# RWKV's output products grouped by tile form, its gram products by turns into two banks of a shared PSUM pool

## The chip, the cores and the metric

One core of a Trainium2 chip runs the program. The metric is the time of one execution on the device in microseconds (us). The kernel before was run three times; one more execution was profiled, and all rows below are from that one.

## The reference

One layer of a hybrid backbone over 2048 latent tokens and 256 context tokens, width 1024: adaLN and norm, one input projection, three token mixers side by side (gated DeltaNet, RG-LRU, RWKV-7; each in both directions over the tokens), one output projection, a squared-ReLU FFN. All in fp32. The mixer that the change touches is RWKV-7, 6 heads of 64 channels, where per token and head the state S (64x64) goes by

```python
def step(S, xt):
    w, kk, a, k, v, r = xt
    S = (S * w[:, :, None, :]
         - jnp.einsum('bhvk,bhk->bhv', S, kk)[..., None] * (kk * a)[:, :, None, :]
         + v[..., :, None] * k[:, :, None, :])
    y = jnp.einsum('bhvk,bhk->bhv', S, r)
    return S, y
```

DeltaNet (GDN below) has a recurrence of the same kind; its keys and queries are normalised per head, and its decays come from gates.

## The kernel before

The kernel runs in four stretches: `front` (the normed tokens h in DRAM, and RWKV's operands), then `middle` with two chains one after the other, then the FFN. The change is in the first half of `middle`: `rwkv_mixer` beside `gdn_features`.

**RWKV's chain.** The recurrence is taken in chunks of 64 tokens, 36 steps per direction, both directions (dd 0 and 1) beside each other. Of a pair of heads each has 64 of the 128 partitions (`half[par]`), so six heads are 3 pairs r by 2 parities par. Per direction and step there are:

- `gram(dd, n)`: loads `pk` (4 operands of 64 tokens per head), and multiplies them with each other: per parity three products of 64 rows, 128 columns each, into a bank `rg` (one PSUM bank, pool `rpg`, one buffer). VectorE takes from it `am` and `zl` (masked), ScalarE `mu`, the matrices to be inverted. 8 grams (4 steps) make a round of 24 units.
- `Lanes.invert`: the inverses of a round, 60 small VectorE operations (`ltmp`, `yl`) in a row between transposes (`ml`, `x`, `y`), and small products (`lmc`, `lmy`) in a bank of the pool `rpl`.
- `load(dd, n)`: `kbr`, scaled on GpSimd and transposed on TensorE to `kbn`.
- `step(dd, n)`: three dependent products in banks `rps` (pool `rpc`, two buffers): z from the state `s` and `zl`, copied to `zz`; u from the inverse `y` and `zz`, copied to `uv`; `ds` from `kbn` and `uv`, added on VectorE to the decayed state `se`. From step 4 on the output follows, `rout` (pool `rpl`): per pair and parity a product of the state `s` with `rt` (a part of `kbr`), 64 rows, and one of `uv` with `am`, 128 rows, summed in PSUM; ScalarE copies it to `o`.

`chains` sets their order: grams up to 16 half-steps ahead, an inverse's parts among the steps of the round before.

**GDN's features.** `gdn_features` streams h three times (keys, queries, values; 9 pieces of 256 tokens) past columns of the input projection: per tile of 128 columns 24 products into a bank `proj` (pool of two), each fp32 operand split in two parts (`hh`, `hl`; `whi`, `wlo`). Then a convolution and SiLU (`gy`), norms over heads by a product with ones (`gssq`), transposes to rows (`nps`). Beside them run `gates`, `decays` (`gdps`, `dm`, `edm`) and `ada_rest` (`adw`, `adps`). Their small products share the pool `gss`, two banks under the tag `sm`.

`weave` sets the two beside each other as the program is written down: half a part of the features to each part of the chain, and what is left of them after the chain. A scheduler then lays the instructions out per engine, each engine taking its own in that fixed order, and hands out the buffers of the pools. The lines of the profile: matmuls are issued by a helper (L156), VectorE's by L130, L135 and L138, ScalarE's activations by L108. PSUM has 8 banks: here 1 (`rpg`), 1 (`rpl`), 2 (`rpc`), 2 (`proj`), 2 (`gss`).

Of the kernel before, what the change touches and what calls it, by code (L numbers as in the profile page):

```python
# [7 lines left out]
F32 = mybir.dt.float32  # L8
# [12 lines left out]
T = SEQ + CTX  # L21
# [16 lines left out]
def poff(p):  # L38
    """column of a piece (256 tokens and its halo) in the padded h."""
    return 0 if p == 0 else 259 + 256 * (p - 1)  # L40


# scratch arrays in DRAM: name -> (shape, dtype)
# [26 lines left out]
class K:  # L70
    """one kernel's context: engines, inputs, scratch, constants."""
# [22 lines left out]
    def col(self, v):  # L94
        """a [128,1] column of a constant."""
        if v not in self.cols:
            t = self.const.tile([128, 1], F32, name=f"col{len(self.cols)}")
            self.G.memset(t, v)
            self.cols[v] = t
        return self.cols[v]  # L100
# [13 lines left out]
    def after(self, a, b):  # L114
        """a comes after b on their engine"""
        self.tc.add_manual_dep(a, b.name, mybir.DependencyInfo(
            mybir.DependencyClass.NoSync, mybir.DependencyReason.DATA), reason="order")

    def table(self, name):
        """the activation tables of what follows, up to the next call; what came before stays before."""  # L120
# [19 lines left out]
    def rms(self, pool, ss, n, eps):  # L140
        """[128, 1]: (ss / n + eps) ** -0.5, by Newton's steps from a guess by the exponent's bits"""
# [16 lines left out]
    def params(self):  # L158
        """vectors over channels as columns: rows of 128 loaded, then transposed by TensorE."""
# [31 lines left out]
# ---------------------------------------------------------------- adaLN modulation and h  # L191
def ada_first(k, pp, tag):
    """silu(c), shift and scale of the mixers' norm as columns, for latent (0) and context (1) tokens."""
# [36 lines left out]
def ada_part(k, j, q, w):  # L230
    """columns of chunk j of ada_w: their products with silu(c) in two sums over 512 rows, yet to be summed over
    the partitions. w: [128, 4, ADA_W] twice"""
# [12 lines left out]
def ada_row(k, j, q, w, acc, ps, gain, out):  # L245
    """the columns with their bias, times a gain, in every partition"""
# [9 lines left out]
def ada_rest(k, p, pp, tag):  # L256
    """scale and shift of the FFN's norm as columns; the mixers' gate times their post norm's gain as rows. In parts."""
# [23 lines left out]
def make_h(k, w, pp, tag):  # L281
    """norm of the tokens, scaled and shifted, channels on partitions. In parts, a piece each, after one that loads the first."""
# [44 lines left out]
# ---------------------------------------------------------------- the input projection  # L327
def split(k, e, src, raw, hi, lo):
    """src -> hi + lo = src exactly, of float32r, by way of raw"""
# [6 lines left out]
class Proj:  # L336
    """tiles of 128 columns of w_in, split in two float32r parts, and pieces of h streamed past them."""
# [8 lines left out]
    def weight(self, i, c0, m):  # L346
        """tile i: m columns from c0; it takes the place of the tile i before"""
# [9 lines left out]
    def raw(self, dtype):  # L357
        """what is to be split, and the second parts of h"""
        return self.hp.tile([128, self.u, PW], dtype, name="hl", bufs=self.lb)

    def weights(self, cols):
        """cols: (first column, how many) of each tile"""
# [4 lines left out]
    def passes(self, sets):  # L367
        """(set, piece, h): every set of tiles past all pieces. After the last piece a tile gives way to the next set's."""
# [13 lines left out]
    def load(self, p):  # L382
        """h of piece p and its halo, in units of channels, each split in two parts."""
# [13 lines left out]
    def parts(self, f, h, a=0, b=PW):  # L397
        """feature tile f of this piece: PSUM [m, b-a]. In parts."""
# [10 lines left out]
    def products(self, ps, f, h, kk, a, b):  # L409
        """what 128 channels of h add to feature tile f"""  # L410
# [5 lines left out]
    def feats(self, fs, h, a=0, b=PW):  # L416
        """several feature tiles beside each other, so that h's first channels are done with early"""
# [7 lines left out]
def drain(parts):  # L425
    """all parts of a computation; what it returns"""
# [7 lines left out]
def rsq(k, out, ps, scale, eps):  # L434
    """out = (scale * ps + eps) ** -0.5"""
# [4 lines left out]
def to_rows(k, pool, work, dst, src, tag):  # L440
    """src [128 (head parity, channel), 3 pairs, 256 tokens] -> rows: dst [(head parity, token of a chunk), 4 chunks,
    (pair, channel)] in DRAM, odd heads first."""
# [11 lines left out]
def backwards(k, rows):  # L454
    """rows(direction) [(head parity, token of a chunk), ...] in DRAM: the second direction's, from the first's"""
# [4 lines left out]
def gdn_features(k, es):  # L460
    """GDN's operands, in passes over h: keys, queries, values. In parts."""
# [5 lines left out]
    sm = es.enter_context(tc.tile_pool(name="gss", bufs=2, space=PSUM, side="right"))  # L467
# [6 lines left out]
    def normed(p, y, sq, s):  # L474
        """divided by the heads' norms; both orders of tokens"""
# [56 lines left out]
def lru_features(k, rec):  # L532
    """RG-LRU's inputs and output gates. In parts."""
# [13 lines left out]
def gdn_gates(k):  # L547
    """twice GDN's output gates. In parts."""
    N = 4
    with ExitStack() as es:  # L550
# [3 lines left out]
        for _, p, h in pj.passes([[(C_Z + 128 * j, 128) for j in range(3)]]):  # L554
            for j in range(3 if p else 0):
# [4 lines left out]
                # together, for the functions of RG-LRU are of other tables by turns  # L560
# [12 lines left out]
def turns(*parts):  # L573
    """parts of several computations by turns"""
# [4 lines left out]
def rwkv_out(k, w, pp, tag):  # L579
    """group norm over the heads, gain and bias, bonus, gate. In parts, by turns without functions of tables and with  # L580
    logarithms and powers."""
# [34 lines left out]
def gates(k):  # L616
    """Rows over tokens, of the heads and directions: (0) the decay's sums gc in chunks of 64, (1) exp(last gc - gc),
    (2) beta, (3) exp(gc). 256 tokens on a partition; the second direction's rows run backwards within each chunk. In parts."""
# [9 lines left out]
    def put(a, dd, x):  # L628
        """the second direction's rows run backwards within each chunk."""
# [1207 lines left out]
```

## Time and profile before

| what | us |
|---|---|
| three runs | 4391.04, 4398.76, 4412.45 |
| median | 4398.76 |
| span of the profiled execution, first to last instruction | 4383.5 |
| PE busy in the span | 3780.3 |
| DVE busy in the span | 2514.7 |
| GpSimd (POOL) busy in the span | 1702.6 |
| ScalarE (ACT) busy in the span | 1632.1 |

The profiled execution's own time is not given apart from its span; the median of the runs lies 15.3 us above that span. PE is TensorE's matmuls, PEld its weight loads, which run beside them; busy time is a union, so instructions that overlap count once. PEclk in a window is the granted clock as a share of 2.4 GHz. In the rows a name as `rout<-kbr,s` reads: written tile, then what is read; idle time before an instruction stands in brackets with what ended it.

### The profile page before, as it was taken

The page shows a single profiled execution, that of the slowest core. Times are in us where ns is not written, and L with a number is a line of the kernel's source. Part 1 is how long each engine was busy: PE and PEld are TensorE (multiplying, and loading weights), DVE is VectorE, ACT ScalarE, POOL GpSimd, SP SyncE. Part 2 cuts the span into 40 slices and gives each one's busy share as a digit, 9 for nine tenths or more (in the row PEclk, how much of TensorE's full clock was granted, in tenths as well). Part 3 has the DMA queues.
Part 4 walks back from the last instruction along what each step waited for, and adds up shares of the span by engine and source line. Part 5 has one row for each costly group of instructions (what it writes and reads, how often), then busy time and mean ns, then how long its engine had stood idle before and what let it go on. Part 6 is the DMA issues. An engine that isn't in the chain of part 4 may idle for free. (4 is left out here: it accounts for less than half of the span.)

```text
span 4383.5 us, 73864 instructions
## 1 busy us (share of the span) xinstructions
PE 3780.3 (86%) x28210; PEld 3119.3 (71%) x28210; DVE 2514.7 (57%) x4815; ACT 1632.1 (37%) x3393; POOL 1702.6 (39%) x1701
## 2 busy tenths in 40 slices
PE   5778786889999897867768768979999999999998
PEld 3667675777778676657556547768888887888886
DVE  3556455686787755329997996643333337333334
ACT  3443443454546433323355534542222214121212
POOL 3323233344356433445558564522233215121212
PEclk8888887888789777879788759989999999999999
DMA  7444446445556554454446465652121214111112
GB/s 208 122 111 110 106 105 172 121 137 149 153 158 197 169 148 127 142 164 119 122 118 189 128 192 152 196 173 64 59 60 60 63 44 151 48 53 44 53 44 82
DMA packets 561887, 527.52 MB, mean 120 GB/s; under 512 B 105069, under 2 KB 515326, under 8 KB 560382
## 3 DMA queue, kind: packets, MB, share of 16 engines
q1 hardware_dynamic: 556414, 506.02, 39.9%
q0 software_dynamic: 5120, 16.78, 1.3%
q8 instruction: 223, 3.65, 0.4%
q14 instruction: 130, 1.06, 0.1%
HBM read 396.87 MB, written 143.49 MB: 123 GB/s over the span
## 5 line engine op out<-in xcount | busy, mean ns | idle before, releaser
L156 PE MATMUL proj<-hh,whi 128*128 128x258 f32 (+2 forms) x2040 | 655.0, 328 | 113.1 <-ACT hh L392 58.7
L156 PE MATMUL proj<-hl,whi 128*128 128x258 f32 (+2 forms) x2040 | 650.2, 321 | 4.2 <-POOL hl L130 4.1
L156 PE MATMUL proj<-hh,wlo 128*128 128x258 f32 (+2 forms) x2040 | 639.0, 315 | 1.2 <-DVE wlo L130 1.2
L130 DVE TENSOR_TENSOR facc<-facc,fdn 128x512 f32<-128x512 f32 x480 | 326.1, 686 | 401.4 <-PE fdn L156 401.4
L156 PEld LDWEIGHTS proj<-hh,whi 128*128 128x128 f32 x2040 | 433.5, 216 | 152.7 <-ACT hh L392 62.7
L156 PEld LDWEIGHTS proj<-hl,whi 128*128 128x128 f32 x2040 | 439.5, 216 | 31.3 <-issue 16.4
L156 PEld LDWEIGHTS proj<-hh,wlo 128*128 128x128 f32 x2040 | 438.9, 216 | 18.0 <-issue 12.2
L130 POOL TENSOR_TENSOR hl<-hl,hh 128x520 fp32r<-128x520 f32 x216 | 291.0, 1353 | 383.3 <-ACT hh L392 293.2
L156 PE MATMUL fup<-fhh,uhi 128*128 128x512 f32 x1024 | 405.1, 396 | 7.5 <-DMA fhr<-h 4.3
L156 PE MATMUL fup<-fhl,uhi 128*128 128x512 f32 x1024 | 403.9, 395 | 0.8 <-DVE fhl L130 0.6
L156 PE MATMUL fup<-fhh,ulo 128*128 128x512 f32 x1024 | 403.8, 394 | 0.0
L156 PE MATMUL fdn<-dhi,ah 128*128 128x512 f32 x1024 | 399.2, 391 | 4.4 <-ACT ah L1743 1.8
L156 PE MATMUL fdn<-dlo,ah 128*128 128x512 f32 x1024 | 399.1, 390 | 0.0
L156 PE MATMUL fdn<-dhi,al 128*128 128x512 f32 x1024 | 395.0, 390 | 0.3 <-DVE al L130 0.3
L130 POOL TENSOR_TENSOR dlo<-draw,dhi 128x1024 fp32r<-128x1024 f32 x32 | 77.5, 2422 | 562.5 <-ACT dhi L331 562.5
L331 ACT CAST dhi<-draw 128x1024 fp32r<-128x1024 f32 x64 | 67.1, 1049 | 567.7 <-PE fdn L156 512.9
L130 POOL TENSOR_TENSOR fq<-fr 128x512 f32<-128x512 f32 x128 | 151.7, 1186 | 325.6 <-ACT fr L108 324.8
L130 DVE TENSOR_TENSOR ltmp<-yl,ml 128x30 f32<-128x30 f32 (+14 forms) x480 | 241.4, 503 | 10.6 <-DVE lu L135 0.8
L130 DVE TENSOR_TENSOR yl<-yl,ltmp 128x30 f32<-128x30 f32 (+14 forms) x480 | 238.6, 497 | 9.1
L156 PEld LDWEIGHTS fup<-fhh,uhi 128*128 128x128 f32 x1024 | 193.2, 189 | 52.7 <-ACT fhh L331 8.7
L392 ACT CAST hh<-hl 128x520 fp32r<-128x520 f32 x216 | 131.2, 623 | 261.4 <-DMA hl<-ht 253.3
L130 DVE TENSOR_TENSOR al<-fq,ah 128x512 fp32r<-128x512 f32 x128 | 93.6, 732 | 234.5 <-ACT ah L1743 234.1
(363 smaller groups left out, 8255.8 us busy)
## 6 DMA issues: line engine op xcount, KB each, us to landing
hl<-ht SPq DMA_DIRECT2D x144, 260.0 KB
uraw<-in_ffn_up_dram SPq DMA_DIRECT2D x64, 512.0 KB
draw<-in_ffn_down_dram SPq DMA_DIRECT2D x64, 512.0 KB
pk<-pk SPq DMA_DIRECT2D x72, 384.0 KB
kbr<-pk SPq DMA_DIRECT2D x72, 288.0 KB
hl<-ht SPq DMA_DIRECT2D x36, 520.0 KB
pk<-pk SPq DMA_DIRECT2D x72, 192.0 KB
pk<-pk SPq DMA_DIRECT2D x18, 768.0 KB
```

The costliest lines, as they stand in the source:

```text
L130: return e.tensor_tensor(out=out, in0=a, in1=b, op=op)
L156: self.last = self.PE.matmul(out, l, r, start=start, stop=stop).ins
L331: k.A.copy(hi, raw)
L392: k.A.copy(hh[:, x, :], raw[:, x, :])
```

## The change

Three things. (1) In `step`, the output's products are written in two groups, first the six of the state (64 rows), then the six of the values (128 rows); the first of the bank starts its sums, the others add where nothing was written since. (2) In `gram`, both parities' banks are taken first, and the products are written by turns between the parities; the readers follow after. (3) The pool `rpg` (one bank) and the pool `gss` (two banks) become one pool `msm` of three banks, opened in `middle`, in which a gram's two banks and all of GDN's small products have the tag `sm`. Comments and docstrings fall away too.

```diff
-def gdn_features(k, es):
+def gdn_features(k, es, sm):
...
-    sm = es.enter_context(tc.tile_pool(name="gss", bufs=2, space=PSUM, side="right"))
...
-def rwkv_mixer(k, es, ln):
+def rwkv_mixer(k, es, ln, psg):
...
-    psg = es.enter_context(tc.tile_pool(name="rpg", bufs=1, space=PSUM))
...
-        ges = []
-        for par in range(2):
+        ges = [psg.tile([128, 3, 128], F32, name=f"rg{par}", tag="sm") for par in range(2)]
+
+        for r in range(3):
+            for h, ge in zip(half, ges):
+                k.mm(ge[:, r, :], pk[h, r, 1:3, :].rearrange("p a t -> p (a t)"), pk[h, r, 0:4:3, :])
+        for par, ge in enumerate(ges):
             h, o = half[par], half[1 - par]
             A.copy(zl[h, par], pk[h, :, 0, :])
-            ge = psg.tile([128, 3, 128], F32, name="rg")
-            for r in range(3):
-                k.mm(ge[:, r, :], pk[h, r, 1:3, :].rearrange("p a t -> p (a t)"), pk[h, r, 0:4:3, :])
-            ges.append(ge)
...
             for r in range(3):
                 for par in range(2):
                     h = half[par]
-                    k.mm(out[h, r, :], s[h, par, r, :], rt[h, r, :], True, False)
-                    k.mm(out[h, r, :], uv[:, par, r, :], am[:, par, r, :], False, True)
+                    k.mm(out[h, r, :], s[h, par, r, :], rt[h, r, :], r == 0, False)
+            for r in range(3):
+                for par in range(2):
+                    k.mm(out[half[par], r, :], uv[:, par, r, :], am[:, par, r, :], False, r == 2)
...
-            weave(k, rwkv_mixer(k, es, ln), gdn_features(k, es), rates[0])
+
+            sm = es.enter_context(k.tc.tile_pool(name="msm", bufs=3, space=PSUM))
+            weave(k, rwkv_mixer(k, es, ln, sm), gdn_features(k, es, sm), rates[0])
```

The built programs show what became of it. PE's order at RWKV's last output, before and then with the change (`s` is the state, `uv` and `am` the values and their matrix):

```order
L156 MATMUL rps<-uv,kbn 64x64 x6
L156 MATMUL proj<-hh,whi_16506 128x260
L156 MATMUL rout<-kbr,s_15452 64x64
L156 MATMUL rout<-am,uv 64x64
L156 MATMUL rout<-kbr,s_15452 64x64
L156 MATMUL rout<-am,uv 64x64
```

```order
L156 MATMUL rps<-uv,kbn 64x64 x6
L156 MATMUL rout<-kbr,s_15449 64x64 x6
L156 MATMUL rout<-am,uv 64x64 x6
L156 MATMUL proj<-hl,whi_12359 128x260
L156 MATMUL proj<-hh,wlo_12360 128x260
```

The two forms stood by turns and now stand in blocks of six. In the new program all 64 outputs have the six of a form before the six of the other; in 37 nothing stands between.

PE's order among the first grams, before and then with the change (the numbers behind rg tell the two banks of a gram apart):

```order
L156 MATMUL rg<-pk 128x128 x6
L156 MATMUL rps<-kd_5694,ork 128x256 x3
L156 MATMUL rg<-pk 128x128 x6
L1439 MATMUL rps<-ident,kbr 128x128 x6
L156 MATMUL rps<-s_5818,zl 64x64 x6
```

```order
L156 MATMUL rg_6072<-pk 128x128
L156 MATMUL rg_6073<-pk 128x128
L156 MATMUL rg_6102<-pk 128x128 x3
L1437 MATMUL rps<-ident,kbr 128x128 x3
L156 MATMUL rg_6103<-pk 128x128 x3
L1437 MATMUL rps<-ident,kbr 128x128 x3
L156 MATMUL rps<-s_5818,zl 64x64 x6
```

Some grams stand by turns, others as three and three with other work between. Of the 72 grams 23 stand by turns (11 of these with nothing between), 48 as three and three, one mixed.

POOL's order behind the last `kbr` of RWKV's chain, before and then with the change (`hl` is the second part of h for proj; `edm`, `dm` are of the decays, `adw` of the modulation; `lx` belongs to the next half of `middle`):

```order
L130 TENSOR_TENSOR kbr<-kbr,wend 128x3x128
L130 TENSOR_TENSOR hl<-hl,hh 128x520 x2
L130 TENSOR_TENSOR se_15585<-s_15438,wend 64x192 x2
L130 TENSOR_TENSOR se_15598<-s_15452,wend 64x192 x2
L130 TENSOR_TENSOR hl<-hl,hh 128x520 x4
L938 MEMSET lx_18138 128x2
```

```order
L130 TENSOR_TENSOR kbr<-kbr,wend 128x3x128
L130 TENSOR_TENSOR se_15460<-s_15311,wend 64x192 x2
L130 TENSOR_TENSOR edm<-dm,neg 128x3x4x64
L236 DMA adw_16107<-in_ada_w_dram 128x4x128
L130 TENSOR_TENSOR hl<-hl,hh 128x520
L130 TENSOR_TENSOR adw_16106<-adw_16106 128x128
L130 TENSOR_TENSOR se_15582<-s_15435,wend 64x192 x2
L130 TENSOR_TENSOR hl<-hl,hh 128x520
L130 TENSOR_TENSOR adw_16106<-adw_16106 128x128
L130 TENSOR_TENSOR dm<-dm,cols 128x768
```

Features that stood among RWKV's steps now stand behind them. Counted over PE's order, proj products ahead of the first product of step 5 are 540 before and 336 with the change (those of the features alone), from there to step 35 1524 and 961, and behind the last rout and ahead of GDN's first gram 126 and 895. Behind the last kbr and ahead of GDN's chain POOL has 56 hl, 54 adw, 14 edm, 13 dm, 17 loads of adw and 4 gsq now.

## Rows read from the trace of the kernel before

**Rows 1.** the page: span and instructions

```profile
span 4383.5 us, 73864 instructions
```

**Rows 2.** windows of all engines; columns: stretch, length, busy (instructions), PEclk, DMA share, GB/s

```profile
706.00:873.00 167.00, 112.68 (x833) 96.48 (x834) 105.19 (x215) 74.81 (x166) 70.11 (x81) 0.72 0.54 150
873.00:977.50 104.50, 90.11 (x934) 78.03 (x934) 85.85 (x181) 53.30 (x122) 50.52 (x62) 0.87 0.48 143
977.50:1500.00 522.50, 492.77 (x4656) 412.18 (x4654) 384.39 (x841) 268.41 (x594) 266.47 (x311) 0.84 0.57 168
1500.00:1865.00 365.00, 300.34 (x2840) 250.04 (x2838) 186.31 (x400) 130.72 (x280) 139.88 (x163) 0.75 0.47 137
1865.00:1910.00 45.00, 28.76 (x204) 24.75 (x204) 12.16 (x26) 13.82 (x24) 16.55 (x16) 0.73 0.58 174
```

**Rows 3.** the same windows, instructions on rout alone (PE, PEld, ACT)

```profile
977.50:1500.00 522.50, 125.76 (x864) 88.72 (x864) 11.44 (x36) 0.84 0.57 168
1500.00:1865.00 365.00, 90.89 (x578) 63.93 (x578) 7.66 (x24) 0.75 0.47 137
```

**Rows 4.** the same windows, instructions on proj alone (PE, PEld, DVE, ACT)

```profile
977.50:1500.00 522.50, 175.67 (x972) 149.73 (x970) 52.99 (x115) 17.32 (x37) 0.84 0.57 168
1500.00:1865.00 365.00, 109.49 (x552) 93.79 (x552) 30.68 (x67) 10.87 (x23) 0.75 0.47 137
```

**Rows 5.** timeline of PE, 1868 to 1872 us; columns: start, us, instruction

```profile
1868.01 0.56 PE L156 MATMUL rps<-zz,y 64*64 64x64 f32 x12
1868.51 0.57 PE L156 MATMUL rps<-uv,kbn 128*64 128x64 f32 x12
1868.90 0.28 PE L156 MATMUL rout<-am,uv 128*64 128x64 f32 x2
1869.11 0.33 PE L156 MATMUL rout<-kbr,s 64*64 64x64 f32 x2
...
1871.42 0.33 PE L156 MATMUL rout<-am,uv 128*64 128x64 f32 x2
```

**Rows 6.** timeline of PE at 1167 us, granted clock 0.50

```profile
1167.41 1.54 PE L156 MATMUL rps<-zz,y 64*64 64x64 f32 x20
1168.87 0.58 PE L156 MATMUL proj<-hh,whi 128*128 128x260 f32 x1
```

**Rows 7.** timeline of PE at 1883 us, granted clock 0.50

```profile
1883.13 0.47 PE L156 MATMUL rout<-kbr,s 64*64 64x64 f32 x2
...
1887.97 0.59 PE L156 MATMUL proj<-hl,whi 128*128 128x260 f32 x1
```

**Rows 8.** windows of all engines around these timelines, columns as in rows 2

```profile
1166.70:1168.90 2.20, 2.20 (x25) 1.86 (x24) 2.06 (x5) 0.45 (x1) 0.00 (x0) 0.50 0.48 124
1883.10:1887.90 4.80, 4.80 (x25) 3.43 (x24) 2.06 (x5) 0.70 (x2) 2.07 (x2) 0.50 0.27 76
1868.00:1872.00 4.00, 4.00 (x49) 3.19 (x49) 1.05 (x3) 0.31 (x1) 0.00 (x0) 1.00 0.57 173
```

**Rows 9.** instructions on tile zz and on tile o: count, ns, first and last start

```profile
L1456 DVE COPY zz<-rps x72: 310/357/360, 753.9 to 1865.3; 128x192 f32<-128x192 f32 x72
...
L1487 ACT COPY o<-rout x64: 297/318/326, 969.7 to 1888.1; 128x192 f32<-128x192 f32 x64
```

**Rows 10.** timeline of DVE at 977.5 us: the eleventh of the copies to zz

```profile
977.46 0.34 DVE L1456 COPY zz<-rps 128x192 f32<-128x192 f32 x1
```

**Rows 11.** waits of PE, 706 to 1910 us: us in total, times, longest

```profile
PE rg L156 <- ACT mu L1411: 72.0, 27, 14.3
```

**Rows 12.** groups of POOL, 706 to 1910 us: busy, mean ns, idle before

```profile
L130 POOL TENSOR_TENSOR hl<-hl,hh 128x520 fp32r<-128x520 f32 x109 | 144.6, 1327 | 157.8 <-ACT hh L392 105.9 <-PE proj L156 16.3 <-ACT gy L108 15.4
...
L130 POOL TENSOR_TENSOR adw<-adw 128x128 f32<-128x128 f32 x144 | 72.4, 512 | 59.8 <-ACT adw L108 56.3
...
L130 POOL TENSOR_TENSOR edm<-dm,neg 128x768 f32<-128x768 f32 x18 | 33.0, 1836 | 0.3
...
L130 POOL TENSOR_TENSOR dm<-dm,cols 128x768 f32<-128x768 f32 x18 | 27.7, 1536 | 23.5 <-DMA dm<-gb 12.5 <-DVE cols L719 10.9
```

## The prediction

> **What bounds the kernel now.** The span is 4383.5 us [rows 1]; the median of the three runs, 4398.76, lies 15.3 above it, and the sum below is made against the span. I read the windows by stretch first. The changed code runs from 706 us, where RWKV's first gram products start, to 1910, where the last of GDN's features is written. What stands before is the same on every engine; what stands after has the same work, slightly interleaved anew. In 706 to 1910 PE is the busiest engine: 94% of 977.5 to 1500 and 82% of 1500 to 1865, against 74% and 51% for DVE [rows 2]. There, then, PE's time is worth nearly its own length, as long as no other engine is as full.
>
> Two things share PE here: RWKV's chain of 36 steps and GDN's features (proj). Two copies to zz mark a step; the first stands at 753.9, the eleventh (step 5) at 977.5, the last two at 1865 [rows 9, 10]. So 30 steps take 887 us, 29.6 each, with 793 us of PE [rows 2], 26.4 a step; 3.1 is idle.
>
> Then the timeline of one output event. A logical fp32 product is two matmuls. Written with the state's product (64 rows) and the values' product (128 rows) by turns, at the full clock (granted 1.00, 2.4 GHz [rows 8]) each logical product takes (1871.42 - 1869.11) / 9 = 0.257 us. Right before it, two groups of the same two forms, six logical products each, take 0.50 (64 rows) and 0.39 us (128 rows) up to the next start [rows 5]. At granted 0.50, which is 1.2 GHz [rows 8], the twelve by turns take 1887.97 - 1883.13 = 4.84 us [rows 7], while one grouped form goes at 1.46 / 20 = 0.073 us a matmul [rows 6].
>
> **The change, part by part.**
>
> *Output products grouped.* An event is 3.08 us at the full clock now (12 x 0.257), 4.84 at half. Grouped it is two blocks of twelve matmuls: at most 2 x 0.50 = 1.0, and at half 24 x 0.073 = 1.75. The 1442 matmuls of rout in the two large windows are 60 events and 216.7 us [rows 3], 3.6 each, which lies 30% of the way from 3.08 to 4.84. So an event becomes 0.7 x 1.0 + 0.3 x 1.75 = 1.23: a saving of 2.4 per event, 4.75 a step (two directions), 142 us in the 30 steps. The new order keeps the blocks whole: in 37 of 64 events all twelve logical products stand together, in every one the six of a form come first.
>
> *Gram by turns.* The by-turn order survives scheduling in only 23 of 72 grams; elsewhere three of one head stand, then three of the other. What two 64-row halves gain by overlapping at 128 columns no row shows. I take nothing; the other bound is half of these products' time, 23 x 12 matmuls x about 0.06 = 15 us. The Trainium skill, "TensorE: Matmul & The Clock Gate", Part 3 on packing, says that weight loads overlap running matmuls only where the row group differs, which is this case in those 23 grams; by it the sum would be those 15 us lower. No row of the trace decides it, and the sum goes without it.
>
> *Two banks for a gram.* Now the second head waits until the first head's readers (am, zl, mu) are done: PE lost 72.0 us in 27 such waits, 2.7 each [rows 11]. With two banks of three this goes, but the pool is shared: a gram takes two, so GDN's small products (gssq, nps, gdps, adps) often find one bank or none. Their matmuls then wait on PE for a gram's readers, with proj and the chain's products queued behind. Bounds: all 72 gained, or as many such waits lost. I take half of the gain, at the start, where the grams come fast.
>
> *What the schedule makes of it.* This is the largest part. In PE's new order features fall behind RWKV: ahead of step 5 stand 336 proj products instead of 540, between steps 5 and 35 961 instead of 1524, after RWKV's last output 895 instead of 126. So the stage splits into a lighter chain and a tail of features alone.
>
> **The sum.** Step pace: proj costs (175.67 + 109.49) / 1524 = 0.187 us a product [rows 4], so 563 fewer take 3.5 us off each step. PE's work falls to 26.4 - 4.75 - 3.5 = 18.2 us a step. DVE has 570.7 / 30 = 19.0 now [rows 2], of it 83.7 / 30 = 2.8 for proj [rows 4]; with 37% of that gone, 18.0. Two engines of 18 that wait for each other by turns don't run at 18. With PE 82 to 86% busy, as in the second and fourth windows [rows 2], it is 21 to 22; with DVE at the 74% of the third, 24. I take 23 (bounds 21 and 26): 30 x 23 = 690 instead of 887, -197. The start to step 5: 204 fewer proj products are 38 us of PE, and some 30 of the gram waits go; but the first inverse (DVE) and the loads bound it too, so I take -40 (bounds 0 and -75). RWKV's last copy then comes at 1888 - 237 = 1651 [rows 9].
>
> The tail: on PE 895 x 0.187 = 167 us at most. But POOL has moved too. Behind its last kbr stand 56 hl (1.327 us), 54 adw (0.512), 14 edm (1.836), 13 dm (1.536) [rows 12], which is 148 us, with 17 adw loads issued by it, 4 gsq and some small ones, about 180 by the groups' means. SP issues 49 loads of h, 37 of and for dm, 32 stores of kv there. I take 185 (bounds 150, PE's part with some cover, and 215, POOL with waits for DMA). End of the stage: 1651 + 185 = 1836 against 1910, **-74 us**. GDN's chain behind it has the same work and starts earlier by that; its new interleaving I cost at nothing (either way by 15): its own waits for DVE set it. 4383.5 - 74 + 15.3 = **4325 us**.
>
> **Rivals.**
>
> *No tail to speak of.* DVE alone sets the pace (18 to 20 us a step) and PE runs the tail in 125 to 150: 30 x 9.6 = -288, start -40, RWKV's end at 1560, stage's end near 1700, -210: 4189. For it: DVE's share was only 74% with PE at 94% [rows 2], so it has room. Against: POOL's 180 us of tail.
>
> *Evacuation and POOL take the gain back.* Each gram still needs am, zl and mu, each step zz, uv and s, in DVE's order behind 30 pairs of inverse operations; at 25 us a step and a tail of 195 (22 stand there now) it is -138 - 40 + 173 = -5, 4394, no change that can be seen. The rule of the Trainium skill on "TensorEngine Tiling (Array Packing)", section PSUM Bottleneck, is this one: tiling speeds up TensorE but not the emptying of PSUM. The trace speaks for it in that DVE's work per step is as long as PE's new one, against it in that PE was the fuller engine in each large window.
>
> *Slower: the shared pool blocks PE.* Its place is PE's queue at gssq and nps. They take two tiles each in 18 units, 72 tiles, and 72 grams take from the same three banks. A wait is worth 2.7 us [rows 11]. It decides from the point where these waits eat the 74 us and 22 more: some 36 waits of that length beyond today's 27, all on PE's path. If half of the 144 allocations wait, 72 x 2.7 = 194, less the 72 gone: +122 against the sum, 4447. Against: the order was laid out with these three banks, and pushed features back rather than into the grams' way.
>
> *It does not do what it says*: true for the grams (23 of 72), and counted so; not for the output products.
>
> **How the numbers follow.** The forecast and its bounds 0.67; no tail 0.13; the gain taken back 0.13; slower 0.07. About 0.5% (22 us) is what a measurement of this kernel can tell from no change. So faster 0.80, same 0.13, slower 0.07. Pace 21 and a tail of 150 give -169, pace 26 with a tail of 215 +46; the range runs from 4230, most of the way to the first, to 4395, into the third case, and leaves out about 2 in 10.
>
> **What would show it.** Right: rout's PE time of 216.7 us in 60 events falls under 90; the waits of rg on mu fall under 30; RWKV's last copy near 1650; then a stretch of some 185 us with proj alone, POOL over 85% and PE under 75% busy; GDN's first gram some 75 us earlier. Wrong: the last copy after 1780; the tail over 230 us; new waits of gssq, nps or rg on am, zl, mu over 70 us; or rout grouped at over 2 us an event, which would mean that the change of form is not what costs 0.257.

## The result and the profile after

The changed kernel takes 4424.28 us (median of 12 runs, 4413.15 to 4436.61) against 4397.43 for the kernel before beside it (12 runs, 4386.90 to 4417.79): ratio 1.0056, 95% interval 1.0037 to 1.0076. The forecast was 4325 us and faster; it is slower by 0.56%, and outside the range of 4230 to 4395.

The page of the changed kernel: the span, the busy tenths of PE and DVE and the granted clock in 40 slices of 110.6 us. The fall of PE to 4 and 5 in the 16th to 18th slice is the stretch that went wrong:

```profile
span 4422.9 us, 73965 instructions
...
PE   5778886788988765448777768989999999999998
...
DVE  3546456979878732118998896643333337333334
...
PEclk8888787778868776669887758999999999999999
```

Its span stands 39.4 us above that of [rows 1]. The same stretches as in [rows 2], cut where the changed kernel has its marks: to step 5, to step 35, and from RWKV's last copy to the last rows of the features. Columns as there.

```profile
706.00:929.00 223.00, 165.49 (x1615) 142.32 (x1613) 182.41 (x391) 105.87 (x247) 90.06 (x105) 0.73 0.54 157
929.00:1575.00 646.00, 541.65 (x6827) 458.58 (x6826) 509.15 (x1109) 314.62 (x724) 297.31 (x370) 0.78 0.54 161
1583.00:1961.00 378.00, 196.21 (x982) 176.31 (x982) 86.76 (x160) 129.40 (x229) 157.32 (x156) 0.67 0.45 129
```

The marks themselves, as in [rows 9, 10]: the tiles zz and o, and the eleventh copy to zz on DVE's timeline.

```profile
L1454 DVE COPY zz<-rps x72: 340/357/359, 763.4 to 1576.6; 128x192 f32<-128x192 f32 x72
L1488 ACT COPY o<-rout x64: 295/318/343, 923.2 to 1582.7; 128x192 f32<-128x192 f32 x64
L1454 DVE COPY zz<-rps x1: 358/358/358, 929.1 to 929.1; 128x192 f32<-128x192 f32 x1
```

So 30 steps take 647.5 us, 21.6 each, where they took 29.6; RWKV's last copy comes at 1582.7 instead of 1888.1, 305 us earlier. And then the features alone need 378 us more, with PE 52% busy, POOL 42%, DVE 23%. First the output products in the 30 steps, to be set against [rows 3]; then proj in the tail, to be set against [rows 4]:

```profile
929.00:1575.00 646.00, 89.73 (x1442) 69.96 (x1440) 19.07 (x60) 0.78 0.54 161
```

```profile
1583.00:1961.00 378.00, 172.47 (x844) 155.53 (x844) 48.92 (x108) 16.56 (x36) 0.67 0.45 129
```

GDN's first gram product, which follows the stage, moves from 1944.7 to 1985.9 (tile gg, before and then after):

```profile
L156 PE MATMUL gg<-kq x864: 218/218/367, 1944.7 to 2571.2; 64*64 64x64 f32 x173
```

```profile
L156 PE MATMUL gg<-kq x864: 218/218/367, 1985.9 to 2613.8; 64*64 64x64 f32 x173
```

From there to the end are 2437.0 us, before 2438.8. All of the loss is made in the tail and carried to the end nearly unchanged. Waits in the tail, all engines (us in total, times, longest):

```profile
DVE gy L138 <- ACT gy L108: 154.8, 23, 19.3
ACT hh L392 <- DMA hl<-ht: 133.3, 21, 16.7
POOL hl L130 <- ACT hh L392: 112.6, 17, 17.4
...
PE proj L156 <- ACT hh L392: 62.7, 8, 15.1
PE proj L156 <- DVE gy L138: 46.8, 17, 11.1
```

Read from the bottom: PE waits for the first part of h (hh), ACT for the load of h, POOL for ACT; and by turns for DVE's convolution (gy), which waits for ACT. It is one file of short steps, each on another engine.

### The profile page after: what moved, and what is told of

Its sections match the earlier page's. It is cut to its first block, busy times and chain, and to the rows that moved or that the text cites. A ratio compares the mean times of both kernels' runs of the same rounds, so it can differ in the third digit from the quotient of the medians.

```text
span 4422.9 us, 73965 instructions
## 1 busy us (share of the span) xinstructions
PE 3674.0 (83%) x28210; PEld 3044.1 (69%) x28210; DVE 2514.8 (57%) x4815; ACT 1631.2 (37%) x3393; POOL 1703.2 (39%) x1701
## 5 line engine op out<-in xcount | busy, mean ns | idle before, releaser
L156 PE MATMUL proj<-hl,whi 128*128 128x258 f32 (+2 forms) x2040 | 659.3, 325 | 27.0 <-POOL hl L130 27.0
L156 PEld LDWEIGHTS proj<-hh,whi 128*128 128x128 f32 x2040 | 442.5, 219 | 242.7 <-ACT hh L392 119.4
L130 DVE TENSOR_TENSOR ltmp<-yl,ml 128x30 f32<-128x30 f32 (+14 forms) x480 | 229.4, 478 | 10.3 <-DVE r L130 0.8
```

What stands on the lines that cost most here:

```text
L130: return e.tensor_tensor(out=out, in0=a, in1=b, op=op)
L156: self.last = self.PE.matmul(out, l, r, start=start, stop=stop).ins
```

## The experiments

Three questions: which part of the change makes the tail, what the tail costs per product, and whether the parts are worth anything without it. In the expectations theory A says that the common tag of grams and GDN's small products pushes the features behind the chain; the other letters are its rivals, with the time that each would give. For every version the number of proj products behind RWKV's last rout is counted in the order of the built program; it is the length of the tail before anything runs. Ratios are to the kernel before, run beside each, with 95% intervals.

### Which part makes the tail

**Grouping alone** (kernel before, output products as in the change; 24 products behind the last rout):

```diff
-                    k.mm(out[h, r, :], s[h, par, r, :], rt[h, r, :], True, False)
-                    k.mm(out[h, r, :], uv[:, par, r, :], am[:, par, r, :], False, True)
+                    k.mm(out[h, r, :], s[h, par, r, :], rt[h, r, :], r == 0, False)
+            for r in range(3):
+                for par in range(2):
+                    k.mm(out[half[par], r, :], uv[:, par, r, :], am[:, par, r, :], False, r == 2)
```

> The kernel before with its output products grouped, and nothing else: own banks for the grams and for GDN's small products, as before. Theory A (the grouping pays, and what is lost is lost in the tail of features, which comes of the shared pool): PE's order has 24 proj products behind RWKV's last output, the stage from 706 to 1910 us ends 90 to 140 us earlier, median 4260 to 4310. Rival B (the two banks and the turns of the grams cost, the tail is only filled differently): the same here, 4260 to 4310. Rival C (PE's time in this stage is not worth anything, for what it gives back turns into other waits, as the changed kernel shows): 4380 to 4415.

4329.79 us, 0.9869 (0.9847 to 0.9891): faster by 1.3%, though 20 us short of what A expected. The grouped form is as cheap here as in the whole change, 84.06 us for 1452 matmuls (first fence), but the steps take 28.7 us. Windows of all engines in the second fence:

```profile
972.00:1832.00 860.00, 84.06 (x1452) 64.94 (x1452) 19.07 (x60) 0.80 0.55 162
```

```profile
972.00:1500.00 528.00, 445.40 (x5005) 382.24 (x5006) 415.09 (x890) 285.28 (x627) 283.94 (x326) 0.83 0.59 175
1500.00:1832.00 332.00, 227.21 (x2557) 199.22 (x2557) 169.69 (x363) 118.21 (x255) 126.68 (x150) 0.75 0.47 142
```

PE falls from 94% to 84% and from 82% to 68% of these stretches [rows 2]: of some 133 us of PE's work on rout saved (216.7 [rows 3] less 84), 57 come back as time; the rest turns into waits.

**Pools and grams alone** (the changed kernel, output products by turns as before; 856 behind).

> The changed kernel with its output products by turns again, as before: gram by turns and shared pool alone. Theory A: 856 proj products stand behind RWKV's last output; RWKV's steps take 25.5 to 27 us instead of 21.5, its last output comes near 1720 us, the tail of features lasts 350 to 390 us as in the changed kernel: 4500 to 4570. Rival B: as long, 4500 to 4570, since the grams are the same. Rival C: as the changed kernel, 4400 to 4450.

4527.07 us, 1.0332 (1.0304 to 1.0361), as A expected. This half of the change alone costs 3.3%; its tail is 363 us.

**The shared tag without turns** (the changed kernel, each parity's gram products written whole before the other's, so one bank at a time; 879 behind):

```diff
-        ges = [psg.tile([128, 3, 128], F32, name=f"rg{par}", tag="sm") for par in range(2)]
-        for r in range(3):
-            for h, ge in zip(half, ges):
-                k.mm(ge[:, r, :], ...
+        for par in range(2):
...
+            ge = psg.tile([128, 3, 128], F32, name="rg", tag="sm")
+            for r in range(3):
+                k.mm(ge[:, r, :], ...
```

> Grouped output products and the pool of three shared, but each gram's two halves one after the other in one bank, as before. Theory A (the shared tag makes the tail): 879 proj products behind RWKV's last output, a tail of 350 to 390 us, 4400 to 4460, as the changed kernel. Rival B (two banks taken at once and the turns make the loss): the tail stays but the chain is not slowed, or the loss goes: under 4350. Rival C: 4390 to 4430.

4433.23 us, 1.0112 (1.0089 to 1.0136): A, not B. The tail comes with the shared tag, without the turns. The change itself, at 1.0056 (1.0037 to 1.0076), is some 0.5% faster than this version, so two banks at once and the turns together gain a little.

**The rate.** `weave` writes half a part of the features to each part of the chain, and the rest behind. With the pools of before the built order at the rate 0.8 is that at 0.5, and at 0.9 it has 61 instead of 126 products behind: the small products of the features have a pool of their own there and are moved ahead. With the common tag they keep their written place behind the grams, and the rate decides. (A version with two banks for grams and one for GDN's own small products, not run, has 541 behind, so having fewer banks does part of it.) The edit is one number:

```diff
-def middle(k, rates=(0.5, 1.0, 0.7)):
+def middle(k, rates=(1.0, 1.0, 0.7)):
```

> The changed kernel with the features written at twice the rate beside RWKV's chain (1.0 parts to each instead of 0.5); same pool, same grams, same products. Theory A: buffers of one tag are handed out in the order in which the program is written, so the features follow the rate; no proj product stands behind RWKV's last output, the tail is gone, the steps take 26 to 28 us, the stage ends near 1790 to 1850 us: 4280 to 4350. Rival B: the grams' pool still costs, 4400 or more. Rival C: 4390 to 4420.

> The changed kernel with the rate 0.8: 386 products behind the chain in the order, between 895 (rate 0.5) and 62 (rate 0.9). Theory A, in proportion (a product costs 0.28 us more in the chain and 0.43 us less in the tail, so 0.144 us net): first GDN product near 1913 us, total 4345 to 4380. If the tail only costs once it is longer than what POOL and TensorE can do (185 us by my sum): no more than at the rate 0.9, 4305 to 4330.

> The changed kernel with GDN's features written at 0.9 pieces of code per piece of RWKV's, not 0.5. The order of TensorE's instructions then has 62 feature products per... (counted as events of the order) behind the last output product instead of 895. Theory A (the tail is what is written behind the chain; a feature product alone costs 0.42 us, amid the chain about 0.33 us): RWKV's last copy near 1850 us, a tail of 25 to 50 us, first GDN product near 1880, total 4320 to 4365 us. Rival R (a higher rate only shifts the same waits into the chain, so that the sum is that of the changed kernel): 4400 to 4430.

Rate 1.0 (none behind): 4333.07, 0.9879 (0.9859 to 0.9900). Rate 0.8 (386 behind): 4342.36, 0.9885 (0.9834 to 0.9935). Rate 0.9 (62 behind): 4316.43, 0.9853 (0.9822 to 0.9885). The totals go A's way; 0.8 and 0.9 come out 3 and 4 us below its bounds. At the rate 1.0 only the total does: in its profile the 30 steps took 31.8 us each, not 26 to 28, and RWKV's last copy came at 1899.8 us, 12 us later than before. That the total still lies in A's range is luck as far as A goes: GDN's first gram product stands ahead of RWKV's end there, at 1859.6 instead of 1944.7 us.

```profile
L1488 ACT COPY o<-rout x64: 295/318/333, 935.6 to 1899.8; 128x192 f32<-128x192 f32 x64
```

```profile
L156 PE MATMUL gg<-kq x864: 218/267/367, 1859.6 to 2535.5; 64*64 64x64 f32 x173
```

At 0.9 the change with nothing altered but the moment at which features are written is 1.5% faster than before instead of 0.6% slower. That is the shown cause: the order, not the products.

### What a product costs in the tail

Tail here is the time from RWKV's last copy to the last store of the features' rows; proj matmuls are those in it. Each row is one profiled execution. The last two columns are PE's own busy time for one and the granted clock.

| version | tail us | proj | us each | PE's own | clock |
|---|---|---|---|---|---|
| the change | 378.4 | 844 | 0.448 | 0.204 | 0.67 |
| pools and grams alone | 363.2 | 812 | 0.447 | 0.202 | 0.66 |
| shared tag, no turns | 374.2 | 805 | 0.465 | 0.204 | 0.66 |
| rate 0.8 | 154.8 | 334 | 0.464 | 0.192 | 0.67 |
| sixth buffer | 355.3 | 830 | 0.428 | 0.194 | 0.69 |
| decays on DVE | 356.8 | 769 | 0.464 | 0.207 | 0.66 |
| scales early | 367.0 | 871 | 0.421 | 0.197 | 0.68 |
| one load | 254.8 | 733 | 0.348 | 0.162 | 0.73 |
| one load, scales early | 218.4 | 736 | 0.297 | 0.148 | 0.76 |
| and a third bank | 217.0 | 691 | 0.314 | 0.143 | 0.72 |
| and decays early, two banks | 231.5 | 914 | 0.253 | 0.145 | 0.79 |

The first four rows differ in length by a factor of 2.5 and have the same price, 0.45 to 0.47 us a product. In the chain a product cost PE 0.187 us [rows 4], and my tail of 185 us for 895 was 0.207.

**One load** of h for all pieces (`load` is called for the first piece only).

```diff
-                if p + 1 < NP or more:
+                if (p + 1 < NP or more) and not getattr(self, "once", False):
                     ahead = self.load((p + 1) % NP)
```

> The changed kernel, but GDN's features load, split and use the first piece of h for all pieces (the loads, casts and splits of the other pieces are left out, and their features are not those of the reference). Theory T1 (in the tail the features wait for their own h: load, cast and split of a piece are not ahead of its products, since five buffers hold the four remainders of a piece and one raw block): the chain of waits gives loads, casts and splits 157 of the tail's 378 us, so the tail falls to 190 to 260 us, total 4240 to 4320. Theory T2 (the tail is set by the convolution, activation and decay chain behind each product, two banks deep): the tail stays above 330 us, total 4375 to 4425.

4265.69 us, 0.9734 (0.9696 to 0.9773); tail 254.8, in T1's range. But fewer products lie in it; per product it is 0.100 us less, 84 us of 378. Loads hold some 22% of the tail's price, not the 157 us that the chain of waits gave them. The proj matmuls of this tail, and its longest waits:

```profile
1538.00:1793.00 255.00, 118.84 (x733) 112.63 (x734) 42.13 (x91) 13.94 (x30) 0.73 0.43 128
```

```profile
DVE gy L138 <- ACT gy L108: 75.9, 18, 14.0
ACT adw L108 <- DMA adw<-in_ada_w_dram: 62.6, 9, 14.8
...
PE adps L156 <- POOL adw L130: 36.0, 5, 13.4
```

With one load gone from the file, another stands in it: adw, the scales for the FFN.

**A sixth buffer** for h and its remainders. A piece has four remainders that stay until its last product, so five buffers leave room for one raw block ahead.

```diff
-    pj = Proj(k, es, "g", u=2, hb=5, raw=5)
+    pj = Proj(k, es, "g", u=2, hb=5, raw=6)
...
-        cols = w.tile([128, 4, 18], F32, name="cols", bufs=2)
+        cols = w.tile([128, 4, 18], F32, name="cols", bufs=1)
```

> The changed kernel with six instead of five buffers for raw blocks and remainders of h (one buffer of a small decay tile given up for the room). T1: one more block of each piece is loaded ahead, one of its four loads with 6.3 us of wait each (133.3 us in 21 waits) over 12 pieces: the tail falls by 20 to 70 us, total 4355 to 4405. T2: no change, 4415 to 4432.

4411.23 us, 1.0066 (1.0039 to 1.0093): the ratio is that of the change. The tail is 23 us shorter in the one profile, 0.020 us a product; the total lies between the two expectations. Inconclusive at this rate.

**Decays on DVE** (dm and edm, `k.tt(V, ...)` for `k.tt(G, ...)`).

> The changed kernel with the two additions of each decay tile (dm, edm: 12 of each in the tail, 41 us) on DVE instead of POOL. Theory T3 (POOL is the tail's queue: the remainders of h stand behind the decays there, and POOL is the busiest engine beside PE with 157 of 378 us): the tail falls by 30 to 60 us, total 4360 to 4395. T1: POOL idles more and the loads set the pace as before, 4405 to 4435.

4418.30 us, 1.0086 (1.0054 to 1.0119), 0.464 us a product: POOL's work in the tail falls from 157 to 111 us, and the price of a product does not fall (0.448 before). T3 falls: POOL, on which my 185 us rested, was not the bound.

**Scales early** (`next(rest, None)` twice per piece), with h loaded as in the change, and then with one load:

> The changed kernel with two steps instead of one of the FFN's scales (tile adw: its own loads, casts and products) beside each piece of features, so that they are done before the tail. Theory T4 (the tail is a single file of short dependent steps, and what stands between two features in the same queues, above all the scales that wait for their load, costs as much as the features' own loads): adw and adps leave the tail, which falls from 378 us to 330 to 360 us although the order has 932 instead of 895 products in it; total 4385 to 4412. If only the loads of h matter: 0.448 us per product as before, total 4418 to 4445.

> Both: h loaded, split and used once (the other pieces' loads, casts and splits are left out, so their features are not those of the reference) and the scales early. T4: the waits for adw that the run with one load showed in its tail (ACT 62.6 us, TensorE 36.0 us) go too; the tail falls from 255 us to 185 to 225 us, 0.26 to 0.29 us per product, total 4195 to 4240. If the features' own chain (convolution, activation, two banks) sets what is left: 0.35 us per product, total 4255 to 4285.

4446.07 us, 1.0123 (1.0073 to 1.0173), and 4292.38, 0.9773 (0.9723 to 0.9823). Half a hit: in the tail a product costs 0.027 and 0.051 us less, but both totals miss T4's ranges, and lie above those of its rival too. What leaves the tail is paid in the chain: with one load RWKV's last copy moves from 1538 to 1599 us.

**A third bank** for proj (and two for the shared pool), on top of one load and early scales:

> As the run with one load and early scales (the loads, casts and splits of all pieces but the first left out, so those features are not the reference's), with three banks for feature products and two for the shared pool. T2 (two banks and the convolution behind them hold what is left of the tail, 0.297 us per product): the tail falls to 0.24 to 0.27 us per product. If the rest is the lower clock and the decays' and rows' single file: 0.285 to 0.31.

4321.36 us, 0.9851 (0.9821 to 0.9881); 0.314 us a product, no gain. T2's range is missed: the longest wait of the run without it, DVE for ACT at gy (86.6 us, first fence), falls to 21.5 us with it (second fence), and the tail is as long; PE waits longer at nps for ACT, which waits for the decays. The third bank was taken from the shared pool, though, and no run has it without that loss, so a gain from it that the smaller pool eats is not excluded.

```profile
DVE gy L138 <- ACT gy L108: 86.6, 20, 18.2
POOL dm L130 <- DMA dm<-gb: 83.9, 7, 18.6
ACT edm L108 <- POOL edm L130: 60.7, 5, 16.3
```

```profile
POOL dm L130 <- DMA dm<-gb: 83.6, 6, 21.8
ACT edm L108 <- POOL edm L130: 82.0, 7, 19.1
...
PE nps L447 <- ACT gy L108: 56.6, 4, 27.9
...
DVE gy L138 <- ACT gy L108: 21.5, 15, 3.4
```

**Decays early** (eight steps of gates and decays a piece instead of two), on one load and early scales:

> As the run with one load and early scales (the loads, casts and splits of all pieces but the first left out, so those features are not the reference's), with eight steps of the gates and decays beside each piece instead of two, so that all decays are made ahead of the tail. Theory T5 (what is left of the tail's price, 0.297 us per product, is the decays: POOL's dm waits for its load of gb 89.0 us, ACT's edm for POOL 68.5 us, and the features' activations and rows stand behind them on ACT, TensorE 38.0 us): 0.17 to 0.24 us per product, near the products' own 0.15. If other single files (activation, rows, table loads) hold it: 0.27 to 0.31.

4348.83 us, 0.9888 (0.9820 to 0.9956); 0.253 us a product, between the two expectations. The decays hold 0.044 us, 37 us of the tail, and again the chain pays. PE's own 0.145 is now more than half of the price; what stays, 0.11 us, is the features' own file (product, convolution, activation, rows), which I did not take apart.

### What the parts are worth without a tail

**Rate 0.9 with the sixth buffer** (none behind), the fastest version; **grouping with the sixth buffer**, pools as before; **the kernel before with the sixth buffer** alone:

> The changed kernel with the rate 0.9 and the sixth buffer for h; no product stands behind the chain in the order. Theory A with T1: the loads of h cost a little within the chain too (ACT waited 107.9 us for them there, mostly covered), total 4290 to 4318, a few us below the run with the rate alone. If loads are covered within the chain: 4308 to 4325.

> The kernel before with grouped outputs and six instead of five buffers for h, its gram and small pools apart. If the shared pool and the grams by turns are worth something by themselves: slower than the fastest version so far (4283.5 us, shared pool, rate 0.9, six buffers), 4295 to 4320. If the fastest version owes its time to the grouping and the buffer alone: 4275 to 4292.

> The kernel before with the sixth buffer for h alone. The last products of features stand close before the chain's end there, and TensorE waits little for h; if loads of h are covered by the chain, within 0.5% of the kernel before, 4365 to 4395. If they cost in the chain as the fastest version suggests (33 us below the same kernel with five buffers): 4335 to 4365.

4283.52 us, 0.9752 (0.9694 to 0.9809); 4315.42, 0.9828 (0.9802 to 0.9854); 4375.18, 0.9978 (0.9961 to 0.9995). The fastest came out 6 us below its range. The first two were not run side by side, so they were run again together:

> The fastest version again (shared pool, grams by turns, grouped outputs, rate 0.9, six buffers), beside the next kernel on one chip: 0.9752 of the kernel before, 0.970 to 0.981, if the shared pool's 32 us over the next kernel are real.

> Grouped outputs and six buffers with the pools of before, again: 0.9828 of the kernel before, 0.980 to 0.9855, and slower than the kernel beside it by 0.4 to 1.0% if the shared pool is worth something by itself; within 0.3% of it if not.

4281.53, 0.9743 (0.9716 to 0.9771), and 4313.09, 0.9817 (0.9794 to 0.9840). Given the rate and the buffer, the shared pool with grams by turns is worth 0.7%, which the slow change had hidden. The rate does not stand between the two: with the pools of before, grouping and six buffers, TensorE's built order is the same at 0.5 and at 0.9. Without the buffer no gain is seen: 0.9853 at the rate 0.9 against 0.9869 for grouping alone, each within the other's interval. The waits of PE between 700 and 1850 us, first with the shared pool and then with the pools of before, go the same way:

```profile
PE rg L156 <- DMA pk<-pk: 23.1, 7, 11.6
...
PE rg L156 <- ACT mu L1409: 22.5, 10, 3.8
```

```profile
PE rg L156 <- ACT mu L1411: 80.7, 38, 14.5
...
PE rg L156 <- DMA pk<-pk: 1.6, 1, 1.6
```

PE waits 58 us less for mu and 22 us more for the loads of pk; the medians differ by 32 us. That the difference in waits makes the difference in time is argued, not shown.

The buffer alone gives the kernel before 0.2%, and the changed kernel at rate 0.9 1.0%; there, however, the order's last 62 products left the tail with it, so the two are not told apart.

## Why the prediction was wrong

By its own steps, in its order.

- **Grouping: right.** "A saving of 2.4 per event", rout under 90: 216.7 us became 89.73 for the same 1442 matmuls, 2.1 per event of the 60. An event now costs 1.50 us instead of the 1.23 forecast. That it is the change of form that costs is not shown by itself: grouping also parts the two products that are summed in the same place, and no run does the one without the other.
- **Gram by turns: counted at nothing, worth some 15 us of PE.** All rg products from 700 to 1910 us took 157.13 us with the shared tag and no turns, 142.00 in the change (first and second fence), at a granted clock of 0.73 and 0.74; two more versions with turns have 136.53 (rate 0.9) and 146.91 (pools and grams alone), and the kernel before, without turns, 159.68. I left this term out for want of a row. The Trainium skill, "TensorE: Matmul & The Clock Gate", Part 3, says that weight loads overlap running products only where the row group differs; that the turns save time agrees with it. That my bound said 15 too is luck: 23 x 12 x 0.06 is 16.6, and no row has 0.06, since a matmul of rg took 0.185 us of PE before (159.68 us for 864), by which half of the time of these 23 grams is 25 us.

```profile
700.00:1910.00 1210.00, 157.13 (x864) 129.10 (x864) 95.44 (x288) 44.86 (x144) 0.73 0.52 152
```

```profile
700.00:1910.00 1210.00, 142.00 (x864) 113.49 (x864) 95.39 (x288) 44.87 (x144) 0.74 0.52 153
```

- **Two banks: right in kind.** PE's waits for mu fell from 72.0 [rows 11] to 13.4, with 22.5 for the loads of pk instead (700 to 1980 us). I took half. It is the pool of three that does it rather than two banks at once: with the shared tag and no turns, one bank at a time, the waits for mu are 8.1 us (second fence; the first is the change). The rival that the shared pool blocks PE did not come: up to step 35 PE waits 4.9 us at nps, and gssq and gdps are not among its longer waits.

```profile
PE rg L156 <- DMA pk<-pk: 22.5, 9, 11.2
PE rps L156 <- DVE zz L1454: 19.2, 17, 3.8
PE rg L156 <- ACT mu L1409: 13.4, 12, 3.3
```

```profile
PE rg L156 <- ACT mu L1409: 8.1, 8, 3.1
```

- **Step pace: too slow.** 23 forecast, 21.6 measured, at PE 84% busy, which is the case "82 to 86%" that I had worked out and passed over. The chain ended 68 us before the 1651 forecast: 42 by the pace, 8 by the start, and 17 because the last copy stands 6 us behind the last copy to zz instead of 23, which the sum had left as it was. The rule of the Trainium skill on "TensorEngine Tiling (Array Packing)", PSUM Bottleneck, on which a rival stood, does not decide here: DVE was 79% busy in the 30 steps and the chain still gained, though with 563 products of features fewer in it.
- **The start:** -48 us against -40.
- **The tail: the failed step.** "I take 185 (bounds 150, PE's part with some cover, and 215, POOL with waits for DMA)." It took 378. The products' own time came near: 172.47 us for 844 against 167 for 895. What failed is that I priced a stretch of dependent work by its fullest engine. No engine was above 52% (POOL, which was to be over 85%, had 42%), and moving a part of POOL's work away left the price as it was. In its place the runs show a price per product that does not depend on the tail's length, 0.45 us, of which PE itself holds 0.20. Taken away one after the other, the loads of h give back 0.10, the scales 0.05 (0.03 with the loads still there), the decays 0.04; PE's own part goes down with them, to 0.145, at a higher granted clock. The last 0.11 us beside it stays unexplained.
- **The end.** +193 in the tail and -68 in the chain put the last rows of features at 1961 instead of 1836. At GDN's first product it is +41 instead of -74 us, and behind it -1.8, which I had costed at nothing: right. The new median lies 1.4 us above the profiled span where the sum took 15.3, so the error of 115 shows as 99. The 15.3 was no fixed cost: where the record has a run's time and its own span, they lie about 2 us apart, so the profiled execution of the kernel before was a quick one.

The count of 895 products behind the chain stood in the prediction, and so did the sign "the tail over 230 us". A hint for the price stood there too: at 706 to 873 us features ran beside the first grams and inverses, ahead of the steps, and PE was only 67% busy [rows 2]. A row of features alone, to price them by, was missing.

## What to carry to other kernels

When two chains share a pool by one tag, the smaller one's instructions keep their written place behind the larger one's; look at how many are left behind its end, and set the rate by which the two are written together anew. Price what then runs alone by its own pace per product, not by its fullest engine; here that pace came only from the runs after. The same change was 0.6% slower as it stood, and 2.6% faster with one number and one buffer altered, so a part that seems to fail may only have met the wrong order.

## What the runs showed of the hardware

PE's clock made the tail dearer than its instructions: a feature product cost PE 0.187 us in the chain [rows 4] and 0.204 in the change's tail. There the granted clock is 0.67, a mean of 1.00 (2.4 GHz) and 0.50 (1.2 GHz). Windows of all engines around two stalls:

```profile
1747.40:1749.60 2.20, 2.20 (x21) 2.20 (x20) 0.00 (x0) 1.37 (x3) 0.00 (x0) 1.00 0.12 47
1749.70:1753.30 3.60, 1.77 (x15) 1.56 (x14) 0.97 (x3) 0.64 (x2) 2.02 (x3) 1.00 0.54 137
1753.30:1755.40 2.10, 1.98 (x10) 1.67 (x10) 0.00 (x0) 0.00 (x0) 1.81 (x2) 0.69 0.74 216
1755.40:1759.30 3.90, 0.00 (x0) 0.00 (x0) 2.15 (x6) 3.80 (x8) 1.89 (x4) 0.50 0.52 146
1759.40:1763.00 3.60, 3.60 (x17) 3.60 (x18) 0.20 (x1) 0.74 (x2) 1.45 (x2) 0.50 0.51 171
```

And PE's timeline there (start, us, instruction, in brackets the wait before it):

```profile
1748.16 0.28 PE L156 MATMUL proj<-hh,whi 128*128 128x260 f32 x1
1748.28 0.29 PE L156 MATMUL proj<-hl,whi 128*128 128x260 f32 x1
...
1753.38 0.39 PE L156 MATMUL proj<-hl,whi 128*128 128x260 f32 x1 [1.92 <-POOL hl L130]
...
1754.72 0.42 PE L156 MATMUL proj<-hl,whi 128*128 128x260 f32 x1
1754.94 0.42 PE L156 MATMUL proj<-hh,wlo 128*128 128x260 f32 x1
1759.35 0.56 PE L156 MATMUL proj<-hh,whi 128*128 128x260 f32 x1 [3.99 <-DVE gy L138]
```

At 1748 us feature products start 0.12 us apart, at 2.4 GHz. PE then stalls for 1.92 us, until the second part of h (hl) is there, and goes on at first at the same clock. Within the next 2.1 us of nearly full work the clock falls: at 1754.7 the products start 0.22 us apart. The longer wait, 3.99 us for gy, comes only after that, and behind it PE works on at 1.2 GHz. So the half pace here followed a stall of about 2 us, in a stretch in which PE worked 1.77 of 3.60 us, and was there before the wait of 4 us: stalls cost their own length, and products behind them cost nearly twice the time.

Over whole tails the granted clock rises with PE's busy share only roughly: 0.67 at 52%, 0.79 where decays, scales and loads were out of the way and PE was 64% busy, but also 0.67 at 45% (rate 0.8) and 0.72 at 52% (third bank).
